# Attention scores in a two-layer encoder kernel: 64-row products become 128-row products

## The chip, the cores and the metric

The kernel runs on one core of one Trainium2 chip. The metric is the device time of one execution in microseconds; lower is better. Before the change three runs gave 1617.46 us in the median (1617.28 to 1620.55).

## What is computed

Two consecutive layers of an encoder over 512 tokens of width 1024. Each layer mixes tokens in three branches, A (neighbourhood attention on an 8 x 64 grid, 6 heads), B (dilated attention, 3 groups of 2 heads) and M (attention into 256 memory tokens, 4 heads), gates and merges them, and then runs a gated MLP with a short convolution. The heads have 64 features. Cut to what matters:

```python
proj = h @ w_in[l]
q_a, k_a, v_a, q_b, k_b, v_b, q_m, gate_pre = jnp.split(proj, splits, axis=-1)
s = jnp.einsum('bhqd,bhrqcd->bhqrc', q_row, k_win) * scale      # A: 8 x 16 neighbours, plus bias
s = jnp.einsum('bhqd,bhqkd->bhqk', qq, kk) * scale + alibi       # B: one group of heads
s = jnp.einsum('bshd,bmhd->bhsm', qh, km) * (HEAD_DIM ** -0.5)   # M
merged = gates[..., 0, :] * (o_a @ w_br_a[l]) + gates[..., 1, :] * (o_b @ w_br_b[l]) + gates[..., 2, :] * (o_m @ w_br_m[l])
x = x + rms_norm(merged @ w_out[l], g_post_mix[l])
u = depthwise_conv_centred(rms_norm(x, g_pre_ffn[l]) @ w_up[l], conv_w[l], conv_b[l])
a, b = jnp.split(u, 2, axis=-1)
x = x + rms_norm((jax.nn.gelu(a) * b) @ w_down[l], g_post_ffn[l])
```

## The kernel before

Activations lie with features on partitions and the 512 tokens along the free axis, in tiles of 128x512. Nearly every product is made in float32 accuracy from operands in two parts, a high part (float32r) and a low part (the rest): high by high, high by low, low by high. So a linear layer over 1024 features is 24 matmuls for each 128 outputs (`linear`, `mm3`). Each weight tile is loaded by SP, its high part is cast by ScalarE (ACT) and its low part is subtracted by VectorE (DVE) or GpSimd (POOL).

Two heads of 64 features share a tile of 128 partitions, rows 0 to 63 and 64 to 127. For the scores, `stack_split` keeps for each head one query tile whose high part lies on the head's own 64 partitions and whose low part lies on the other 64. `twice_split` keeps for each head one key tile with the high part on both halves (the second half is copied by POOL), and one tile for both heads with the low parts, each on its own half. `mm_stacked` (line 265) then makes a score in two matmuls into the same PSUM bank:

```python
mm(ps, q, k, True, False, cost)     # 128 rows: (high q, low q) by (high k, high k)
mm(ps, qh, kl, False, True, cost)   # 64 rows: high q by low k
```

It is called in `a_head_job` (line 529; two blocks of two pairs for each head, 256 keys each), in `m_head_job` (two blocks of two pairs for each head, 256 keys) and in `b_job` (four blocks for each head, one pair over 512 keys). In `b_job` two more score products in plain float32 stand behind the pair, one for each strided group, over 64 rows and 128 keys (`mm1`); their queries are one tile for both heads, made in `b_q` (line 576).

The order of PE is one stream. `Woven` holds a main stream (the linear layers, one K tile at a time) and jobs beside it (heads, transposes, norms); a job's next part is issued into the main stream as soon as a rough count of the time so far says that its operands should be ready. The order is fixed when the program is built: `Woven.pe` makes every matmul depend on the one before. The counts take a matmul's columns, not its rows, so a switch between shapes has no place in them.

Buffers: `mp` has 35 tiles of 128x512 (tag m), for merged branches, attention operands, the first w_up weights and the MLP's activations; tag `ka` has 9 tiles, for branch A's keys, branch M's queries, the first w_out weights and the MLP's last activations. A new tile waits until the last reader of the buffer's former tile is done. PSUM has eight banks: three for the linear layers (mm), two for scores (s), two for transposes (pt), one for outputs (o). At the end of a sub-layer (`sublayer_end`) the last products are made half by half of the tokens, and the norm of the first half runs beside the products of the second; meanwhile the first six weights of w_up are loaded and split into tiles of `mp` (`group_weights`, low parts on POOL).

Of the kernel before, what the change touches and what calls it, by code (L numbers as in the profile page):

```python
# [16 lines left out]
N_MEM = 256  # L17
# [13 lines left out]
# columns of the per-feature vectors  # L31
# [14 lines left out]
class Woven:  # L46
    """Issue order of the tensor engine: one main stream, and beside it jobs whose parts come as soon
    as the other engines should have their operands ready (by a rough count of the time so far)."""
# [50 lines left out]
class Counted:  # L99
    """An engine, with a rough count of when it is done with what it was given so far."""  # L100
# [19 lines left out]
def tile_hybrid_encoder(ctx, tc, xT, memT, memg, vecs, rpb, w_in, w_kv, w_bra, w_brb, w_brm,  # L120
# [6 lines left out]
    mp = ctx.enter_context(tc.tile_pool(name="mp", bufs=35))  # L127
# [22 lines left out]
    def ktile(dt=F32R, shape=(128, 512)):  # L150
        return tp.tile(list(shape), dt, tag="ka", name=nm("ka"), bufs=9)
# [63 lines left out]
    def behind(ins, other):  # L215
        """Issue ins behind other, of the same engine."""
        if other is not None and ins is not other:
            tc.add_manual_dep(ins, other.name, ORDER, reason="issue order")
# [5 lines left out]
    def weights(src, K, C, slot=None, eng=None, after=None):  # L224
        """An operand of weights in two parts: a list over its K tiles."""
        raw = wp.tile([128, K, C], F32, tag="wraw", name=nm("wraw"))
        nc.sync.dma_start(out=raw, in_=src)
        if slot is None:
            hi = wp.tile([128, K, C], F32R, tag="whi", name=nm("whi"), bufs=2)
            lo = wp.tile([128, K, C], F32R, tag="wlo", name=nm("wlo"), bufs=2)  # L230
            split(raw, hi, lo, eng)
            behind(last_copy[0], after)
            return [(hi[:, k, :], lo[:, k, :]) for k in range(K)]
        n = 512 // C
        w = []
        for k in range(0, K, n):
            c = min(n, K - k)
            hi, lo = slot(F32R, (128, c, C)), slot(F32R, (128, c, C))
            split(raw[:, k:k + c, :], hi, lo, eng)
            w += [(hi[:, i, :], lo[:, i, :]) for i in range(c)]  # L240
        return w
# [23 lines left out]
    def mm_stacked(ps, q, k, qh, kl, n):  # L265
        """q k in float32's accuracy: high and low part of q on top of each other, against the high part of k
        twice, and the high part of q against the low part of k."""
        cost = n / 2400.0
        mm(ps, q, k, True, False, cost)
        mm(ps, qh, kl, False, True, cost)  # L270
# [8 lines left out]
    def stack_split(ps, tiles, scale=None, pv=lambda t: t, tv=lambda t: t):  # L279
        """One tile for each of the two heads in ps: high part on the head's partitions, low part on the others."""  # L280
        for t, row in zip(tiles, (0, 64)):
            part(tv(t[row:row + 64]), tv(t[64 - row:128 - row]), pv(ps[row:row + 64]), scale)

    def twice_split(ps, tiles, lo, scale=None, eng=None):
        """The high part of each of the two heads in ps on both halves of its tile, and the low parts in lo."""
        for t, row in zip(tiles, (0, 64)):
            a = t[row:row + 64]
            part(a, lo[row:row + 64], ps[row:row + 64], scale)
            if eng is None:
                ACT.activation(t[64 - row:128 - row], ps[row:row + 64], AF.Copy, scale=scale or 1.0)  # L290
            else:
                eng.tensor_copy(t[64 - row:128 - row], a)
# [31 lines left out]
    def rstd_job(accs, n, box):  # L324
        """1 / sqrt(mean of squares + eps) of each token, on all partitions (in PSUM)."""
        nb = n // 128
        bank = tbank((128, n + nb))
        pr, pt = bank[:, 0:n], bank[:, n:n + nb]
        for i, a in enumerate(accs):
            for b in range(nb):  # L330
                mm(pt[:, b:b + 1], a[:, 128 * b:128 * b + 128], mean, i == 0 and b == 0,
                   i == len(accs) - 1 and b == nb - 1, 0.11)
        rs = smalls(nb)
        crit[0] = ACT.activation(rs, pt, AF.Sqrt, bias=eps, scale=1.0).ins
        V.reciprocal(rs, rs)
        diag = small("h32", 4, (128, n))
        for b in range(nb):
            V.tensor_scalar_mul(diag[:, 128 * b:128 * b + 128], ident, rs[:, b:b + 1])
        yield 1.2
        mm(pr, ones, diag, True, True, n * 4 / 2400.0)  # L340
        box.append(pr)
# [67 lines left out]
    def mem_kv(l, hm, km, vm, pre=()):  # L409
        wv.need(f"mem{l}")  # L410
        kl = big(F32R, (128, 2, N_MEM))
        for m in range(4):
            w = pre[m] if pre else weights(w_kv[l, m], KD, 128)
            ps = mmbank((128, N_MEM))
            linear(ps, w, hm, slice(0, N_MEM))
            if m < 2:
                t = big(F32R, (128, 2, N_MEM))
                twice_split(ps, (t[:, 0, :], t[:, 1, :]), kl[:, m, :], None, MDUP)
                km.append((t, kl[:, m, :]))
            else:  # L420
                vT = big(F32, (128, 256))
                ACT.copy(vT, ps)
                wv.spawn(mem_v_job(l, vT, vm))

# [26 lines left out]
    def v_split(srcs):  # L451
        """Values of four tiles of keys: for each tile and head the high part beside the low part."""
        ps = tbank((128, 2, 2, 2, 64))
        transposes(ps.rearrange("p a b c d -> p (a b c d)"), srcs)
        out = []
        for a in range(2):
            t = big(F32R, (128, 2, 2, 2, 64))
            split(ps[:, a], t[:, :, :, 0, :], t[:, :, :, 1, :])
            out += [[t[:, b, c] for c in range(2)] for b in range(2)]
        return out  # L460

    def mm_values(po, v, p, cols, first, last, n, view=lambda t: t):
        """Adds v p to the columns of po: high and low part of v against the high part of p (in two halves of
        partitions), and the high part of v against the low part of p."""
# [32 lines left out]
    def a_k(ps, qkv):  # L497
        kk = [ktile(F32R, (128, 528)) for _ in range(3)]
        for t in kk:
            nc.gpsimd.tensor_copy(t[:, 0:8], zero)  # L500
            nc.gpsimd.tensor_copy(t[:, 520:528], zero)
        twice_split(ps, [t[:, 8:520] for t in kk[:2]], kk[2][:, 8:520], -0.125, DUP)
        qkv[1].append(kk)

    def a_v(ps, qkv, flag):
        # columns rolled by 8, then cut in tiles of 16 columns
# [8 lines left out]
    def kwin(t, b):  # L515
        # columns 16 b - 8 to 16 b + 23 of each row, in the order (tile, row, column)
# [12 lines left out]
    def a_head_job(l, h, qkv, neg, oa):  # L529
        qs, ks, vs = qkv  # L530
        pr, row = h // 2, 64 * (h % 2)
        q, k, kl = qs[pr][h % 2], ks[pr][h % 2], ks[pr][2][row:row + 64, :]
        P = []
        for bp in range(2):
            s = sbank((128, 2, 256))
            for b2 in range(2):
                b = 2 * bp + b2
                qsl = slice(128 * b, 128 * b + 128)
                mm_stacked(s[:, b2, :], q[:, qsl], kwin(k, b), q[row:row + 64, qsl], kwin(kl, b), 256)
# [36 lines left out]
    def b_q(g, ps, qkv):  # L576
        if g > 0:
            t = big(F32)
            ACT.activation(r3(t), b_cls(ps), AF.Copy, scale=-0.125)
            qkv[0].append(t)  # L580
            return
# [4 lines left out]
    def b_k(g, ps, qkv):  # L586
# [5 lines left out]
        kk = [big() for _ in range(3)]  # L592
        twice_split(ps, kk[:2], kk[2], None, DUP)
# [10 lines left out]
    def b_job(l, sl, cp, qkv, po, ob):  # L604
# [3 lines left out]
        for c2 in range(2):  # L608
# [4 lines left out]
            mm_stacked(s0, qs[0][sl][:, rsl], ks[0][sl], qs[0][sl][row:row + 64, rsl], ks[0][2][row:row + 64, :], 512)  # L613
# [4 lines left out]
            for g in (1, 2):  # L618
                mm1(s1[:, g - 1, :], qs[g][row:row + 64, rsl], ks[g][row:row + 64, rsl], True, True, 128)
# [42 lines left out]
    def m_head_job(l, h, qm, km, vm, om):  # L662
        pr, row = h // 2, 64 * (h % 2)
        q, (kt2, kl) = qm[pr][h % 2], km[pr]
        P = []
        for qp in range(2):
            s = sbank((128, 2, 256))
            for q2 in range(2):
                qsl = slice(128 * (2 * qp + q2), 128 * (2 * qp + q2) + 128)
                mm_stacked(s[:, q2, :], q[:, qsl], kt2[:, h % 2, :], q[row:row + 64, qsl], kl[row:row + 64, :], 256)  # L670
# [69 lines left out]
    def sublayer_end(l, goff, w_of, rhs, n_half, then, lat=(1.4, 1.8), mid=None):  # L740
        """A sub-layer's last linear layer and its norm. The last n_half output tiles are made half by
        half: the norms of the first half run beside the products of the second."""
# [63 lines left out]
    for l in range(depth):  # L806
# [52 lines left out]
        for j in range(NFF):  # L859
# [13 lines left out]
            hi, lo = (big if j < 18 else ktile)(), (big if j < 17 else ktile)()  # L873
# [45 lines left out]
def _consts():  # L919
# [4 lines left out]
    # query (i, cc) of column block b; key (t, r, c): column 16 (b + t) - 8 + c  # L924
# [24 lines left out]
def _layout(inputs):  # L949
# [19 lines left out]
    # relative position bias by query (i, cc) and key (t, r, c); columns out of the table padded  # L969
# [40 lines left out]
```

## Time and profile before

| | |
|---|---|
| runs, median (lowest to highest) | 1617.46 us (1617.28 to 1620.55) |
| span of the profiled execution | 1616.8 us |
| layer 0: attention, branches A, B, M | 82 to 270 us |
| layer 0: gates and branch projections | 270 to 392 us |
| layer 0: w_out, norm, first w_up tiles | 392 to 462 us |
| layer 1: attention | 880 to 1068 us |
| mean granted TensorE clock | 0.990 |

The span goes from the first to the last instruction of the one profiled execution; the runs' times hold some 0.7 us around it. A row of instructions by form gives line, engine, operation, tile written and tiles read, rows*columns of the weight, shape of the moving operand, count, then busy time in us and mean duration in ns of one. Matmuls overlap, so the mean duration of one is longer than the distance from one start to the next. All matmuls have line 244, as one helper records them; their tiles tell them apart: s are scores, pt transposes, o outputs of attention, mm linear layers. A row in order of time gives start, duration, engine, line, operation, tiles and count.

### The profile page before, as it was taken

The page shows a single profiled execution, that of the slowest core. Times are in us where ns is not written, and L with a number is a line of the kernel's source. Part 1 is how long each engine was busy: PE and PEld are TensorE (multiplying, and loading weights), DVE is VectorE, ACT ScalarE, POOL GpSimd, SP SyncE. Part 2 cuts the span into 40 slices and gives each one's busy share as a digit, 9 for nine tenths or more (in the row PEclk, how much of TensorE's full clock was granted, in tenths as well). Part 3 has the DMA queues.
Part 4 walks back from the last instruction along what each step waited for, and adds up shares of the span by engine and source line. Part 5 has one row for each costly group of instructions (what it writes and reads, how often), then busy time and mean ns, then how long its engine had stood idle before and what let it go on. Part 6 is the DMA issues. An engine that isn't in the chain of part 4 may idle for free.

```text
span 1616.8 us, 21319 instructions
## 1 busy us (share of the span) xinstructions
PE 1571.7 (97%) x8246; PEld 1331.6 (82%) x8246; DVE 916.9 (57%) x1654; ACT 726.2 (45%) x1285; POOL 165.9 (10%) x200
## 2 busy tenths in 40 slices
PE   6999999999999999999989999999999999999997
PEld 5977877889898888878888787778898888888887
DVE  6676566335676565542386746653448665655233
ACT  5455566235444444432344545652354544444231
POOL 4230000110300000010151300001112000000000
PEclk9999999999999999999999999999999999999998
DMA  7221212324202223333331211132331123232331
GB/s 236 85 76 58 67 55 64 111 78 157 79 27 95 100 92 104 112 92 97 121 103 46 76 62 63 48 103 79 104 131 66 53 93 104 91 105 85 98 107 63
DMA packets 46614, 144.95 MB, mean 90 GB/s; under 512 B 5233, under 2 KB 11377, under 8 KB 46513
## 3 DMA queue, kind: packets, MB, share of 16 engines
q1 hardware_dynamic: 44656, 139.61, 26.3%
q10 hardware_dynamic: 1152, 2.10, 0.5%
q0 software_dynamic: 704, 1.88, 0.4%
q8 instruction: 65, 1.06, 0.3%
q14 instruction: 37, 0.30, 0.1%
HBM read 141.47 MB, written 2.10 MB: 89 GB/s over the span
## 4 chain that ended last, share of the span: by engine, by line
PE 92%; DVE 5%; ACT 1%; issue 1%; DMA 0%; SPq 0%; ACTq 0%
PE mm L244 75%; PE s L244 9%; PE o L244 4%; PE pt L244 3%; PE pt L255 2%; DVE h L114 1%; DVE y L114 1%; DVE x L114 1%; DVE acc L114 1%; DMA x<-in_xT_dram 0%; DVE wlo L114 0%; ACT whi L114 0%; ACT sq L114 0%; DVE m L114 0%; ACT y L114 0%
## 5 line engine op out<-in xcount | busy, mean ns | idle before, releaser
L244 PE MATMUL mm<-h,whi 128*128 128x512 f32 x2432 | 758.5, 393 | 0.0
L244 PEld LDWEIGHTS mm<-h,whi 128*128 128x128 f32 x2432 | 449.2, 188 | 93.5
L114 DVE TENSOR_TENSOR wlo<-wraw,whi 128x1024 fp32r<-128x1024 f32 (+1 forms) x203 | 247.4, 1220 | 401.9 <-ACT whi L114 398.2
L244 PE MATMUL mm<-h,wlo 128*128 128x512 f32 x1216 | 473.8, 390 | 0.0
L114 ACT CAST whi<-wraw 128x1024 fp32r<-128x1024 f32 (+1 forms) x203 | 210.4, 1039 | 306.1 <-PE mm L244 301.7
L244 PEld LDWEIGHTS mm<-h,wlo 128*128 128x128 f32 x1216 | 228.3, 188 | 48.8
L244 PE MATMUL mm<-m,whi 128*128 128x512 f32 (+1 forms) x711 | 192.8, 358 | 1.6 <-DVE m L114 0.8
L244 PEld LDWEIGHTS mm<-m,whi 128*128 128x128 f32 x711 | 128.4, 194 | 20.7 <-PE mm L244 1.3
L244 PE MATMUL mm<-m,wlo 128*128 128x512 f32 (+1 forms) x362 | 128.9, 356 | 0.7 <-DVE wlo L114 0.7
L114 DVE SCALAR_TENSOR_TENSOR y<-mm,vec,y 128x511 f32<-128x511 f32 x160 | 118.9, 747 | 8.5 <-ACT y L114 5.9
L114 ACT ACTIVATE y<-mm,vec 128x512 f32<-128x512 f32 (+1 forms) x163 | 113.6, 698 | 0.1
L244 PE MATMUL mm<-m,m 128*128 128x512 f32 (+1 forms) x432 | 89.2, 347 | 0.0
L727 POOL TENSOR_TENSOR m<-m,y 128x512 f32<-128x512 f32 x28 | 36.1, 1288 | 466.1 <-DVE y L114 466.1
L222 POOL TENSOR_TENSOR m<-wraw,m 128x512 fp32r<-128x512 f32 x42 | 57.1, 1374 | 242.4 <-ACT m L114 182.7
L244 PEld LDWEIGHTS mm<-m,wlo 128*128 128x128 f32 x362 | 70.1, 194 | 10.4 <-DVE wlo L114 1.1
L244 PEld LDWEIGHTS mm<-m,m 128*128 128x128 f32 x432 | 67.6, 189 | 9.1
L244 PE MATMUL mm<-h,m 128*128 128x256 f32 x456 | 66.0, 303 | 5.5 <-ACT y L114 2.3
L114 DVE TENSOR_TENSOR acc<-acc,sq 128x256 f32<-128x256 f32 (+1 forms) x86 | 47.2, 551 | 36.9 <-ACT sq L114 36.2
L244 PEld LDWEIGHTS mm<-h,m 128*128 128x128 f32 x456 | 61.4, 206 | 8.1 <-ACT h L114 2.7
L114 ACT ACTIVATE y<-y 128x512 f32<-128x512 f32 x44 | 27.9, 633 | 87.3 <-DVE y L114 87.3
L114 ACT CAST m<-wraw 128x512 fp32r<-128x512 f32 (+1 forms) x98 | 56.1, 602 | 22.0 <-DMA wraw<-in_w_brb_dram 9.7
L114 ACT CAST m<-y 128x512 fp32r<-128x512 f32 x36 | 22.4, 621 | 87.7 <-DVE y L114 87.7
(148 smaller groups left out, 1835.9 us busy)
## 6 DMA issues: line engine op xcount, KB each, us to landing
wraw<-in_w_in_dram SPq DMA_DIRECT2D x88, 512.0 KB, 3.2
wraw<-in_w_up_dram SPq DMA_DIRECT2D x88, 512.0 KB, 3.2
wraw<-in_w_down_dram SPq DMA_DIRECT2D x32, 512.0 KB, 3.5
wraw<-in_w_out_dram SPq DMA_DIRECT2D x16, 512.0 KB, 3.3
wraw<-in_w_down_dram SPq DMA_DIRECT2D x16, 384.0 KB, 3.1
wraw<-in_w_kv_dram SPq DMA_DIRECT2D x8, 512.0 KB, 3.5
wraw<-in_w_bra_dram SPq DMA_DIRECT2D x16, 192.0 KB, 2.3
x<-in_xT_dram SPq DMA_DIRECT2D x8, 256.0 KB, 7.0
```

Of the source, the lines that this page charges most:

```text
L114: return op(*args, **kw)
L222: last_lo[eng or V] = (eng or V).tensor_sub(lo, src, f32(hi)).ins
L244: wv.pe(nc.tensor.matmul(ps, a, b, start=first, stop=last), cost)
L255: wv.pe(nc.tensor.transpose(ps[:, 128 * i:128 * i + 128], s, ident), 0.11)
L727: (V if br == 2 and m >= 6 else G).tensor_add(acc[m], acc[m], gs)
```

## The change

The low part of the keys gets a tile of its own for each head, with the same values on both partition halves, as the high part has it. The second matmul of `mm_stacked` then takes the whole query tile (high and low part) instead of its 64 high rows: 128 rows by 128 rows. It adds low q by low k, which was left out before. For the strided groups of branch B each head gets a query tile of its own whose other 64 rows are zero, so that these products too run over 128 rows; the keys stay one tile for both heads. The buffers are shared out anew: 32 tiles in `mp`, 12 under `ka`, and the MLP's activations from tile 16 on lie under `ka`. Comments are dropped too.

```diff
-    mp = ctx.enter_context(tc.tile_pool(name="mp", bufs=35))
+    mp = ctx.enter_context(tc.tile_pool(name="mp", bufs=32))
...
-        return tp.tile(list(shape), dt, tag="ka", name=nm("ka"), bufs=9)
+        return tp.tile(list(shape), dt, tag="ka", name=nm("ka"), bufs=12)
...
-    def mm_stacked(ps, q, k, qh, kl, n):
+    def mm_stacked(ps, q, kh, kl, n):
         cost = n / 2400.0
-        mm(ps, q, k, True, False, cost)
-        mm(ps, qh, kl, False, True, cost)
+        mm(ps, q, kh, True, False, cost)
+        mm(ps, q, kl, False, True, cost)
...
-    def twice_split(ps, tiles, lo, scale=None, eng=None):
-        for t, row in zip(tiles, (0, 64)):
-            a = t[row:row + 64]
-            part(a, lo[row:row + 64], ps[row:row + 64], scale)
-            if eng is None:
-                ACT.activation(t[64 - row:128 - row], ps[row:row + 64], AF.Copy, scale=scale or 1.0)
-            else:
-                eng.tensor_copy(t[64 - row:128 - row], a)
+    def twice_split(ps, his, los, scale=None, eng=None):
+        for hi, lo, row in zip(his, los, (0, 64)):
+            own, other = slice(row, row + 64), slice(64 - row, 128 - row)
+            part(hi[own], lo[own], ps[own], scale)
+            eng.tensor_copy(hi[other], hi[own])
+            eng.tensor_copy(lo[other], lo[own])
...
     def a_k(ps, qkv):
-        kk = [ktile(F32R, (128, 528)) for _ in range(3)]
+        kk = [ktile(F32R, (128, 528)) for _ in range(4)]
...
     def b_q(g, ps, qkv):
         if g > 0:
-            t = big(F32)
-            ACT.activation(r3(t), b_cls(ps), AF.Copy, scale=-0.125)
-            qkv[0].append(t)
+            tiles = (big(F32), big(F32))
+            for t, row in zip(tiles, (0, 64)):
+                G.memset(t[64 - row:128 - row, :], 0.0)
+                ACT.activation(r3(t[row:row + 64]), b_cls(ps[row:row + 64]), AF.Copy, scale=-0.125)
+            qkv[0].append(tiles)
...
-                mm1(s1[:, g - 1, :], qs[g][row:row + 64, rsl], ks[g][row:row + 64, rsl], True, True, 128)
+                mm1(s1[:, g - 1, :], qs[g][sl][:, rsl], ks[g][:, rsl], True, True, 128)
...
-            hi, lo = (big if j < 18 else ktile)(), (big if j < 17 else ktile)()
+            hi, lo = (big if j < 16 else ktile)(), (big if j < 16 else ktile)()
```

On PE nothing changes its place. These are the rows of the first score block of branch B in layer 0 (s is the score bank, the first m behind the arrow the keys, the second the queries), before:

```order
L244 MATMUL s_1863<-m_1318,m_1209 128x512
L244 MATMUL s_1863<-m_1320,m_1209 128x512
L244 MATMUL s_1869<-m_1590,m_1518 128x128
L244 MATMUL s_1869<-m_1785,m_1752 128x128
L244 MATMUL mm_1894<-h_110,whi_1890 128x512
```

and with the change:

```order
L244 MATMUL s_1894<-m_1338,m_1229 128x512
L244 MATMUL s_1894<-m_1340,m_1229 128x512
L244 MATMUL s_1900<-m_1617,m_1541 128x128
L244 MATMUL s_1900<-m_1816,m_1779 128x128
L244 MATMUL mm_1925<-h_110,whi_1921 128x512
```

The sizes are those of what is written, so the rows read the same; the second, third and fourth product now take 128 rows in place of 64.

On POOL, around the last biases of branch A's heads in layer 0 (rpb are the bias tables, L526 makes a head's bias, L292 copies the keys of branch B), before:

```order
L292 COPY m_1318<-m_1318 64x512
L526 TENSOR_TENSOR y_1371<-mask,y_1371 128x256
L292 COPY m_1319<-m_1319 64x512
L523 DMA y_1495<-in_rpb_dram 128x256
L526 TENSOR_TENSOR y_1494<-mask,y_1495 128x256 x2
```

and with the change (L290 copies the high part, L291 the low part, L579 fills with zeros):

```order
L290 COPY m_1338<-m_1338 64x512
L525 TENSOR_TENSOR y_1394<-mask,y_1394 128x256
L291 COPY m_1340<-m_1340 64x512
L290 COPY m_1339<-m_1339 64x512
L291 COPY m_1341<-m_1341 64x512
L522 DMA y_1518<-in_rpb_dram 128x256
L525 TENSOR_TENSOR y_1517<-mask,y_1518 128x256 x2
L525 TENSOR_TENSOR y_1518<-mask,y_1518 128x256
L579 MEMSET m_1541 64x512
L579 MEMSET m_1542 64x512
```

Behind each copy of a high part now stands one of a low part, and the fills for branch B's queries come behind the last bias.

On ACT, in the second half of w_out of layer 0 (sq and y belong to the norm that follows w_out, m<-wraw are casts of weights), before:

```order
L114 ACTIVATE sq_831_3764<-mm_3739 128x256
L114 ACTIVATE y_3603<-mm_3739,vec 128x256
L114 CAST m_4235<-wraw_4233 128x512
L114 CAST m_4239<-wraw_4233 128x512
L114 ACTIVATE sq_833_3793<-s_3768 128x256
```

and with the change:

```order
L114 ACTIVATE sq_846_3911<-mm_3886 128x256
L114 ACTIVATE y_3638<-mm_3886,vec 128x256
L114 ACTIVATE sq_848_3940<-s_3915 128x256
L114 ACTIVATE y_3639<-s_3915,vec 128x256
L114 CAST m_4266<-wraw_4264 128x512
L114 ACTIVATE st_3966<-pt_3963,eps 128x2
L114 CAST m_4270<-wraw_4264 128x512
```

The casts of the first w_up weight moved behind the sums of squares of w_out's tiles, to the first norm's square root, and the other w_up weights move back by as much.

More of the change, by code (lines that the diff above doesn't have):

```diff
@@ L410, in mem_kv @@
         wv.need(f"mem{l}")
-        kl = big(F32R, (128, 2, N_MEM))
         for m in range(4):
@@ L416, in mem_kv @@
             if m < 2:
-                t = big(F32R, (128, 2, N_MEM))
-                twice_split(ps, (t[:, 0, :], t[:, 1, :]), kl[:, m, :], None, MDUP)
-                km.append((t, kl[:, m, :]))
+                t, u = big(F32R, (128, 2, N_MEM)), big(F32R, (128, 2, N_MEM))
+                twice_split(ps, (t[:, 0, :], t[:, 1, :]), (u[:, 0, :], u[:, 1, :]), None, MDUP)
+                km.append((t, u))
             else:
@@ L501, in a_k @@
             nc.gpsimd.tensor_copy(t[:, 520:528], zero)
-        twice_split(ps, [t[:, 8:520] for t in kk[:2]], kk[2][:, 8:520], -0.125, DUP)
+        inner = [t[:, 8:520] for t in kk]
+        twice_split(ps, inner[:2], inner[2:], -0.125, DUP)
         qkv[1].append(kk)
@@ L531, in a_head_job @@
         pr, row = h // 2, 64 * (h % 2)
-        q, k, kl = qs[pr][h % 2], ks[pr][h % 2], ks[pr][2][row:row + 64, :]
+        q, k, kl = qs[pr][h % 2], ks[pr][h % 2], ks[pr][2 + h % 2]
         P = []
@@ L538, in a_head_job @@
                 qsl = slice(128 * b, 128 * b + 128)
-                mm_stacked(s[:, b2, :], q[:, qsl], kwin(k, b), q[row:row + 64, qsl], kwin(kl, b), 256)
+                mm_stacked(s[:, b2, :], q[:, qsl], kwin(k, b), kwin(kl, b), 256)
             S = ytile((128, 2, 256))
@@ L591, in b_k @@
             return
-        kk = [big() for _ in range(3)]
-        twice_split(ps, kk[:2], kk[2], None, DUP)
+        kk = [big() for _ in range(4)]
+        twice_split(ps, kk[:2], kk[2:], None, DUP)
         qkv[1].append(kk)
@@ L612, in b_job @@
             s0 = sbank()
-            mm_stacked(s0, qs[0][sl][:, rsl], ks[0][sl], qs[0][sl][row:row + 64, rsl], ks[0][2][row:row + 64, :], 512)
+            mm_stacked(s0, qs[0][sl][:, rsl], ks[0][sl], ks[0][2 + sl], 512)
             m0, m1 = smalls(1), smalls(1)
@@ L663, in m_head_job @@
         pr, row = h // 2, 64 * (h % 2)
-        q, (kt2, kl) = qm[pr][h % 2], km[pr]
+        q, (kh, kl) = qm[pr][h % 2], km[pr]
         P = []
@@ L669, in m_head_job @@
                 qsl = slice(128 * (2 * qp + q2), 128 * (2 * qp + q2) + 128)
-                mm_stacked(s[:, q2, :], q[:, qsl], kt2[:, h % 2, :], q[row:row + 64, qsl], kl[row:row + 64, :], 256)
+                mm_stacked(s[:, q2, :], q[:, qsl], kh[:, h % 2, :], kl[:, h % 2, :], 256)
             m = smalls(2)
```

## The prediction

> **What bounds the kernel now.** I read the page first (busy time, chain), then the windows of the attention stages, then PE's products by form, then the order of time around single score blocks.
>
> ```profile
> span 1616.8 us, 21319 instructions
> PE 1571.7 (97%) x8246; PEld 1331.6 (82%) x8246; DVE 916.9 (57%) x1654; ACT 726.2 (45%) x1285; POOL 165.9 (10%) x200
> PE 92%; DVE 5%; ACT 1%; issue 1%; DMA 0%; SPq 0%; ACTq 0%
> 82.00:160.00 78.00, 77.91 (x378) 61.04 (x379) 54.26 (x146) 43.06 (x98) 15.67 (x19) 1.00 0.19 66
> 160.00:235.00 75.00, 75.00 (x384) 59.84 (x383) 42.08 (x104) 41.31 (x75) 0.00 (x0) 1.00 0.19 62
> 235.00:270.00 35.00, 35.00 (x156) 25.62 (x155) 24.63 (x59) 24.25 (x53) 0.00 (x0) 1.00 0.17 52
> ```
>
> The reader is to see that PE (TensorE) is the bound: 97% busy, 92% of the chain that ended last. The three windows (columns: length, then busy time of PE, PEld, DVE, ACT, POOL, then granted clock and DMA) are branches A, B and M of layer 0's attention; layer 1 repeats them. PE has no gap there, the clock is 1.00, and VectorE (DVE) is at 70%, 56% and 70%. So time taken off PE in these stages comes off the span, until a wait takes its place.
>
> But a busy PE need not be PE at its rate. By form, over the whole program:
>
> ```profile
> L244 PE MATMUL s<-h,m 128*128 128x256 f32 x384 | 49.0, 287 | 0.0
> L244 PE MATMUL s<-ka,m 128*128 128x256 f32 x48 | 16.5, 344 | 0.0
> L244 PE MATMUL s<-ka,m 64*128 64x256 f32 x48 | 18.3, 382 | 0.0
> L244 PE MATMUL s<-m,ka 64*128 64x256 f32 x32 | 12.2, 381 | 0.0
> L244 PE MATMUL s<-m,m 64*128 64x512 f32 x16 | 7.9, 495 | 0.0
> L244 PE MATMUL s<-m,m 64*128 64x128 f32 x64 | 9.9, 274 | 0.0
> ```
>
> A product of 256 columns takes 287 ns where all have 128 rows (first row); the score products of 64 rows take 381 and 382, and in branch A their 128-row partners 344. Fewer rows cost more, and the neighbour pays too. That is the sign of a switch between 64-row and 128-row products, not of an operand.
>
> **What a switch costs.** Three blocks of scores in the order of time (start, duration), one for each branch, with the products of the main stream behind them; under them two rows that give the undisturbed rates.
>
> ```profile
> 83.79 1.23 PE L244 MATMUL s<-ka,m 128*128 128x256 f32 x4
> 84.94 0.73 PE L244 MATMUL mm<-h,whi 128*128 128x512 f32 x2
> 85.52 0.40 PE L244 MATMUL mm<-h,wlo 128*128 128x512 f32 x1
> ...
> 174.34 1.27 PE L244 MATMUL s<-m,m 128*128 128x512 f32 x6
> 175.53 0.73 PE L244 MATMUL mm<-h,whi 128*128 128x512 f32 x2
> 176.11 0.39 PE L244 MATMUL mm<-h,wlo 128*128 128x512 f32 x1
> ...
> 235.36 1.21 PE L244 MATMUL s<-m,ka 128*128 128x256 f32 x4
> 236.50 0.72 PE L244 MATMUL mm<-h,whi 128*128 128x512 f32 x2
> 237.07 0.40 PE L244 MATMUL mm<-h,wlo 128*128 128x512 f32 x1
> ```
> ```profile
> 157.68 14.29 PE mm L244 x63
> 447.27 5.76 PE s L244 x48
> ```
>
> Undisturbed, a product of 512 columns starts each 14.29/63 = 0.227 us, and one of 256 each 5.76/48 = 0.120. For 128 columns: the 64 records above stand in 16 runs of four, so (9.9 - 16 x 0.274)/48 = 0.115 from one to the next.
>
> - Branch A: four score products and the two behind them take 85.52 - 83.79 = 1.73; undisturbed 4 x 0.120 + 2 x 0.227 = 0.93. Excess 0.80, four switches, 0.20 each.
> - Branch M: 237.07 - 235.36 = 1.71 against 0.93. Excess 0.78.
> - Branch B, whose 64-row products stand together: 176.11 - 174.34 = 1.77 against 2 x 0.227 + 4 x 0.115 + 2 x 0.227 = 1.37. Excess 0.40, two switches.
>
> **The change, part by part.** All score products get 128 rows, in the same order on PE. The 48, 32 and 16 products of the rows above are 24 blocks of A and 16 of M (two such products each) and 16 of B (one). Taken off PE: 24 x 0.80 + 16 x 0.78 + 16 x 0.40 = 19.2 + 12.5 + 6.4 = **38.1 us**. That a 128-row product with as many columns costs no more follows from the first row against those of 64 rows; I take the difference as nothing, and what is left of an operand's own cost is inside the spread of 0.02 between A and M.
>
> The measured 0.20 us has a rule beside it. The Trainium skill, TensorEngine Tiling (Array Packing), Key Properties, says that a change of tiling mode drains the TensorE, and the Trainium skill, TensorE: Matmul & The Clock Gate, Single matmul latency, gives a constant of 166 ns at full clock that a stream of matmuls hides. An estimate by that figure of the Trainium skill: 24 x 4 + 16 x 4 + 16 x 2 = 192 switches x 0.166 = 31.9 us and a time of 1589; by the rows above it is 38.1, and these decide.
>
> A rule also speaks against the change. The Trainium skill, TensorEngine Tiling (Array Packing), When to Use Tiling, would split a contraction of up to 64 into row tiles that run together; an estimate by it: the 80 products of 256 columns could at best halve, 80 x 0.120 / 2 = 4.8 us, and padding gives this up. The trace shows no two of them side by side, so nothing is lost here.
>
> *Copies and zeros on POOL.* Per layer 8 copies of 64x512, 4 of 64x256, 4 fills of 64x512 and 6 small casts come in.
>
> ```profile
> L292 POOL CAST ka<-ka 64x512 fp32r<-64x512 f32 x12 | 7.6, 632 | 65.5 <-ACT ka L114 65.4
> L292 POOL CAST m<-m 64x512 fp32r<-64x512 f32 x4 | 4.2, 1053 | 3.7 <-ACT m L114 3.5
> 49.40 0.61 POOL L292 CAST ka<-ka 64x512 fp32r<-64x512 f32 x1 [0.67 <-ACT ka L114]
> ```
>
> Copies cost 0.63 to 1.05 us each; a fill has no row of its size, so from nothing to 1.05. Together at most 22 x 1.05 = 23 us a layer on an engine with 15.7 us of work in the first 78 us and none in the next 110. A pair's copies come long before their use (49.40 against the first score at 83.79), so I cost them at nothing. Without that cover, one copy late is about 1 us of PE. The two extra ACT instructions a layer for the queries (about 1 us each at most, by the 64x512 rows above) lie in a stage with ACT at 55%.
>
> *Three buffers fewer in the pool of 128x512 tiles.* With 35, one w_up weight was split while w_out still ran; with 32 (16 merged tiles and 16 of w_out fill the pool) POOL's first subtractions must wait.
>
> ```profile
> 397.60 1.30 POOL L222 TENSOR_TENSOR m<-wraw,m 128x512 fp32r<-128x512 f32 x1 [22.10 <-ACT m L114]
> 410.77 1.28 POOL L222 TENSOR_TENSOR m<-wraw,m 128x512 fp32r<-128x512 f32 x1 [11.88 <-DVE acc L114]
> 437.69 4.17 POOL L222 TENSOR_TENSOR m<-wraw,m 128x512 fp32r<-128x512 f32 x3 [11.48 <-PE mm L244]
> 452.87 0.52 PE L244 MATMUL o<-h,m 128*128 128x256 f32 x3
> ```
>
> The one of 397.60 moves behind 410.77, and one more joins the three at 437.69: done by 437.7 + 4 x 1.39 = 443.3. Queued behind are only the other w_up subtractions, whose last pair is read from 452.87 on: 9 us of cover, so nothing; uncovered it would cost at most the slip, 13 us a layer. Of ACT's casts that move with them, two land next to the norm that follows w_out: between nothing and, by POOL's row, 1.3 us each; I take nothing, as ACT is at 45% overall.
>
> **What is late next.** The scores have two PSUM banks, which VectorE empties. In branch B it is already late:
>
> ```profile
> 184.97 1.27 PE L244 MATMUL s<-m,m 128*128 128x512 f32 x6
> 187.31 1.48 PE L244 MATMUL s<-m,m 128*128 128x512 f32 x6
> 210.06 1.37 PE L244 MATMUL s<-m,m 128*128 128x512 f32 x6
> 185.54 0.69 DVE L114 TENSOR_TENSOR m<-pt,m 128x512 fp32r<-128x512 f32 x1
> 186.15 0.68 DVE L114 CUSTOM_DVE_ANT_0 y<-s,tab 128x512 f32<-128x512 f32 x1
> 186.87 0.69 DVE L114 SCALAR_TENSOR_TENSOR ka<-mm,ka 64x512 fp32r<-64x512 f32 x1
> 187.59 0.42 DVE L114 CUSTOM_DVE_ANT_0 y<-s,tab 128x256 f32<-128x256 f32 x1
> ```
>
> The same six products take 1.27, then 1.48 and 1.37 us, since they wait for the second reading of a bank (187.59), with VectorE busy without a break before it. Between those two blocks the saving (0.40, and half of the next block's, 0.2) turns into a wait at 187.31, and half as much at 210.06: 0.9 us a layer. In branch M VectorE's 24.63 us will stand in 35 - 8 x 0.78 = 28.8 (86%), ScalarE's 24.25 too (84%); I put 0.9 us a layer there, an estimate between nothing and the whole 6.2. Given back in all: 2 x 1.8 = **3.6 us**.
>
> **Sum.** 38.1 - 3.6 = 34.5 us. Span 1616.8 becomes 1582.3; the runs' median, 1617.46, lies 0.7 above the span, so 1583.0.
>
> **Rivals.**
> 1. *VectorE and ScalarE take PE's place in A and M.* For: 86% and 84% dense in M, and the softmax of one head must end before its transposes. Against: no wait there now, and both have over 4 us idle left in M. If half the saving of A and M turned into waits: (19.2 + 12.5)/2 + 1.8 = 17.7 given back, 1597 us.
> 2. *The change doesn't do what it says*: the excess belongs to the second product of an accumulation, not to its rows. Then nothing is gained: 1617 to 1618. Against: the 128-row product behind a block pays as well, and B's row of 64-row products runs at 0.115 inside.
> 3. *Slower: the granted clock falls* as PE loses its pauses in the attention stages, 2 x 187 - 38 = 336 us of PE. It decides from a clock of 336/(336 + 34.5) = 0.91 on; at 0.85 it costs 59 us, 1642 us. Against: the clock is 1.00 where PE is full, and lower where it has gaps:
>
> ```profile
> 427.00:462.00 35.00, 33.53 (x249) 32.70 (x250) 25.09 (x65) 14.43 (x41) 4.10 (x3) 0.91 0.09 31
> ```
>
> **Chances.** Forecast (given back 0 to 8 us, 1579 to 1587) 0.81; rival 1 (1588 to 1606) 0.13; rival 2 0.03; rival 3 0.03. Faster by over 0.2%, which is about what can be told from no change: 0.94; within it 0.03; slower 0.03. The range goes from 1577 (nothing given back, 1579.4, less 2 us for the 0.02 to 0.04 by which 56 blocks may differ) to 1596, which takes in most of rival 1.
>
> **What would show it.** No form with 64 rows among the scores; 256-column scores at 0.28 to 0.29 us as in the first row; a block in A or M of 0.93 us up to the third product behind it. Layer 0's attention 17 to 19 us shorter. The waits that come in stand ahead of the scores in B, released by VectorE. POOL's w_up subtractions start near 411, with the first w_up products not later than before against the norm. Wrong would be: scores of 128 rows that still take over 0.34 us; a clock under 1.00 in attention; gaps of PE in A or M that sum to over 8 us.

## The result, and the profile after

The changed kernel took 1578.80 us in the median (1578.59 to 1579.04), the kernel before, on the same chip, 1617.37: a ratio of 0.9757 with a 95% interval from 0.9738 to 0.9775. The predicted 1583.0 us lay 4.2 us above. The profiled execution took 1579.04 us, with a span of 1577.3.

The page of the profile after: the span, the busy times, and the shares of the chain that ended last.

```profile
span 1577.3 us, 21375 instructions
PE 1529.7 (97%) x8246; PEld 1316.4 (83%) x8246; DVE 911.2 (58%) x1654; ACT 727.4 (46%) x1289; POOL 186.4 (12%) x244
PE 88%; DVE 8%; ACT 2%; issue 1%; DMA 1%; SPq 0%; ACTq 0%
```

The span fell by 39.5 us and PE's busy time by 42.0, with as many matmuls. PE still bounds the kernel, but its share of the chain went from 92% to 88%, and DVE's from 5% to 8%: some of what PE gave up is now waiting.

The windows of branches A, B and M of layer 0 after the change. They are cut where the same matmuls start as at 82, 160, 235 and 270 us before, so the length (second column) compares with 78, 75 and 35.

```profile
81.27:150.20 68.93, 68.83 (x378) 58.67 (x379) 54.48 (x146) 43.86 (x100) 20.64 (x27) 1.00 0.23 74
150.20:222.93 72.73, 71.92 (x384) 59.57 (x383) 41.85 (x104) 41.32 (x75) 0.00 (x0) 1.00 0.21 63
222.93:253.27 30.34, 29.27 (x156) 24.00 (x155) 24.35 (x59) 24.44 (x53) 0.00 (x0) 1.00 0.21 61
```

A is 9.07 us shorter, B 2.27, M 4.66: 16.0 us in layer 0. Layer 1, cut in the same way, is 15.9 us shorter. PE's busy time fell by 9.08, 3.08 and 5.73; where a length fell by less than that, PE now waits, 0.81 us in B and 1.07 us in M.

The scores by form, over the whole program (column in the middle: busy us, mean ns).

```profile
L244 PE MATMUL s<-ka,m 128*128 128x256 f32 x96 | 15.9, 288 | 0.0
L244 PE MATMUL s<-m,ka 128*128 128x256 f32 x160 | 24.8, 284 | 0.0
L244 PE MATMUL s<-m,m 128*128 128x512 f32 x32 | 10.3, 404 | 0.7 <-DVE st L114 0.7
L244 PE MATMUL s<-m,m 128*128 128x128 f32 x64 | 9.9, 277 | 0.9 <-DVE st L114 0.9
```

No score has 64 rows any more. Of branch A's keys (ka) the second products took 382 ns and the first 344; now all 96 take 288. The 64-row products of 512 columns took 495; now all 32 of that size take 404.

The same three blocks in the order of time, after the change, each with the third product behind it.

```profile
83.05 0.64 PE L244 MATMUL s<-ka,m 128*128 128x256 f32 x4
...
83.99 0.39 PE L244 MATMUL mm<-h,wlo 128*128 128x512 f32 x1
...
164.51 1.06 PE L244 MATMUL s<-m,m 128*128 128x512 f32 x6
...
165.87 0.39 PE L244 MATMUL mm<-h,wlo 128*128 128x512 f32 x1
...
223.38 0.63 PE L244 MATMUL s<-m,ka 128*128 128x256 f32 x4
...
224.31 0.39 PE L244 MATMUL mm<-h,wlo 128*128 128x512 f32 x1
```

From the block's start to the third product behind it A takes 0.94 us, B 1.36 and M 0.93. The prediction had reckoned 0.93, 1.37 and 0.93 for blocks without a switch.

Outside the attention stages the span fell by another 39.5 - 31.9 = 7.6 us, for which the prediction had nothing. (In a second pair of profiles, at the end of the next section, this is 4.9.) The next section takes both parts apart.

### The profile page after: what moved, and what is told of

The parts are those of the page before. It is cut to its first block, busy times and chain, and to the rows that moved or that the text cites. A ratio compares the mean times of both kernels' runs of the same rounds, so it can differ in the third digit from the quotient of the medians.

```text
span 1577.3 us, 21375 instructions
## 1 busy us (share of the span) xinstructions
PE 1529.7 (97%) x8246; PEld 1316.4 (83%) x8246; DVE 911.2 (58%) x1654; ACT 727.4 (46%) x1289; POOL 186.4 (12%) x244
## 4 chain that ended last, share of the span: by engine, by line
PE 88%; DVE 8%; ACT 2%; issue 1%; DMA 1%; SPq 0%; ACTq 0%
PE mm L244 73%; PE s L244 6%; PE o L244 3%; PE pt L244 2%; DVE h L114 2%; PE pt L255 2%; DVE y L114 2%; DVE x L114 1%; DVE m L114 1%; DVE wlo L114 1%; ACT whi L114 1%; DVE acc L114 1%; DVE ka L114 0%; ACT y L114 0%; DMA m<-in_memT_dram 0%
## 5 line engine op out<-in xcount | busy, mean ns | idle before, releaser
L244 PE MATMUL mm<-m,whi 128*128 128x512 f32 (+1 forms) x672 | 178.2, 354 | 1.6 <-DVE m L114 0.8
L244 PEld LDWEIGHTS mm<-m,whi 128*128 128x128 f32 x672 | 119.6, 192 | 19.0 <-PE mm L244 1.3
L244 PE MATMUL mm<-m,wlo 128*128 128x512 f32 (+1 forms) x336 | 118.3, 352 | 0.7 <-DVE wlo L114 0.7
L244 PEld LDWEIGHTS mm<-m,wlo 128*128 128x128 f32 x336 | 64.4, 192 | 9.4 <-DVE wlo L114 1.1
L114 ACT CAST m<-pt 128x512 fp32r<-128x512 f32 (+1 forms) x72 | 38.2, 539 | 40.4 <-PE pt L255 32.0
```

What stands on the lines that cost most here:

```text
L114: return op(*args, **kw)
L244: wv.pe(nc.tensor.matmul(ps, a, b, start=first, stop=last), cost)
```

## The experiments

"Gain" is counted against the kernel before, 1617 to 1619 us in each set of runs. Stage lengths are measured between the starts of the same matmuls in two traces.

**The second product on 64 rows again.** The changed kernel, but the low part of the keys is multiplied with the high part of the queries alone (qr, 64 rows), as before; low q by low k is left out. Buffers, copies and padded queries of the strided groups stay.

```diff
-        mm(ps, q, kl, False, True, cost)
+        mm(ps, qr, kl, False, True, cost)
```

> This kernel is the changed one with its copies, zeros and buffers, but the second product of every score pair takes 64 rows again (low query by low key is left out, as before). Theory 1, each switch between 64-row and 128-row products costs 0.20 us of TensorE: A and M have four switches a block again and B two, so attention is as long as before, 16 us more in each layer, and the time is 1611 us (1608 to 1614), since what the change gained outside attention stays. Rival, the gain comes from the new buffers or from where the copies stand: 1579 to 1583 us.

Measured: 1611.38 us, ratio 0.9956 (0.9940 to 0.9971). Each branch of both layers is within 0.2 us of its length before, and the old duration is back:

```profile
L244 PE MATMUL s<-ka,m 64*128 64x256 f32 x48 | 18.4, 383 | 0.0
```

So the whole gain inside attention needs the second product on 128 rows; what is left, 5.8 us, lies outside attention.

**The buffers alone.** The kernel before with the new sizes of the pools and nothing else.

```diff
-    mp ... bufs=35
+    mp ... bufs=32
...
-        ... tag="ka", ... bufs=9)
+        ... tag="ka", ... bufs=12)
...
-            hi, lo = (big if j < 18 else ktile)(), (big if j < 17 else ktile)()
+            hi, lo = (big if j < 16 else ktile)(), (big if j < 16 else ktile)()
```

> The kernel before with the buffers of the changed one (32 tiles in mp, 12 under ka, the MLP's last activations under ka) and nothing else. Theory 1: attention keeps its length (branches A, B and M 188 us in each layer); only the norm behind w_out moves, as GpSimd's subtractions start later: its wait at 427.6 falls from 3.4 to about 2.3 us, time 1612 to 1617 us. Rival, the buffers carry the gain: 1579 to 1590 us.

Measured: 1613.78 us, ratio 0.9972 (0.9958 to 0.9986). Attention keeps its length; most of what moved lies in the w_out stages and at the layer boundary. The profiled execution was the fastest of the ten (1610.05 us), with a mean granted clock of 0.996 against 0.990 in the profile before, so part of its gain is clock. At one mean clock, 0.994, two of these runs have spans of 1610.3 and 1610.4 us and two of the kernel before 1612.5 and 1613.3: some 2.5 us that the clock does not explain. So the new buffer sizes alone made the kernel a little faster. The run changes both pools; which of the two matters is not shown.

**Half as many switches.** The kernel before with its 64-row products kept, but in A and M a block's two 128-row products stand together and then its two 64-row ones: two switches a block where there were four. The cut shows A; M is changed in the same way.

```diff
             for b2 in range(2):
                 b = 2 * bp + b2
-                qsl = slice(128 * b, 128 * b + 128)
-                mm_stacked(s[:, b2, :], q[:, qsl], kwin(k, b), q[row:row + 64, qsl], kwin(kl, b), 256)
+                mm(s[:, b2, :], q[:, 128 * b:128 * b + 128], kwin(k, b), b2 == 0, False, 256 / 2400.0)
+            for b2 in range(2):
+                b = 2 * bp + b2
+                mm(s[:, b2, :], q[row:row + 64, 128 * b:128 * b + 128], kwin(kl, b), False, b2 == 1, 256 / 2400.0)
...
```

> The kernel before, but in each block of branches A and M the two 128-row products come first and then the two 64-row ones: as many 64-row products, two switches in place of four. Theory 1: 40 blocks x 2 x 0.20 = 16 us less, with 2 to 4 us given back to VectorE: 1604 us (1600 to 1607). Rival, a 64-row product is slow by itself or the second product of a pair pays: no gain, 1615 to 1619 us.

Measured: 1601.36 us, ratio 0.9890 (0.9870 to 0.9911). Branch A's first block, and the windows of A, B and M of layer 0, in this kernel:

```profile
83.97 0.83 PE L244 MATMUL s<-ka,m 128*128 128x256 f32 x4
...
85.29 0.40 PE L244 MATMUL mm<-h,wlo 128*128 128x512 f32 x1
```
```profile
82.18:155.65 73.47, 73.38 (x378) 59.92 (x379) 54.23 (x146) 43.00 (x98) 15.69 (x19) 1.00 0.20 70
155.65:230.59 74.94, 74.94 (x384) 59.73 (x383) 42.08 (x104) 41.20 (x75) 0.00 (x0) 1.00 0.18 61
230.59:262.65 32.06, 32.06 (x156) 24.93 (x155) 24.46 (x59) 24.22 (x53) 0.00 (x0) 1.00 0.19 62
```

The block's excess is 85.29 - 83.97 - 0.93 = 0.39 us in place of 0.80. A is 4.53 us shorter and M 2.94, half of the PE time that the change takes off there (9.08 and 5.73), and B, which was not touched, keeps its length. The same products with half the switches cost half the excess: it belongs to the switch, neither to the 64 rows as such nor to the second product of an accumulation. Per switch taken away that is 4.53/24 = 0.19 us in A and 2.94/16 = 0.18 in M.

**The strided groups on 64 rows again.** The changed kernel without the padded queries of branch B.

```diff
-                mm1(s1[:, g - 1, :], qs[g][sl][:, rsl], ks[g][:, rsl], True, True, 128)
+                mm1(s1[:, g - 1, :], qs[g][row:row + 64, rsl], ks[g][row:row + 64, rsl], True, True, 128)
```

> The changed kernel, but the strided groups of branch B keep one query tile and 64 rows, as before. Theory 1: a block of B has its two switches again, so branch B is as long as before, 2.3 to 2.6 us more in each layer: 1583.6 us (1582.5 to 1585). Rival, the rows count and not the switches: the 64-row products of 512 columns are gone all the same, so a third to half of B's gain stays, 1581 to 1582 us.

Measured: 1584.06 us, ratio 0.9786 (0.9759 to 0.9813). Branch B of layer 0 in this kernel:

```profile
151.91:226.82 74.91, 74.87 (x384) 59.62 (x383) 42.02 (x104) 41.21 (x75) 0.00 (x0) 1.00 0.18 61
```

A and M keep their whole gain (9.07 and 4.65 us in layer 0) and B's is gone (75.00 to 74.91): the switch had only moved, from in front of the second product to behind it. So each branch's gain is its own, and B needs all its scores on 128 rows to get anything.

**Later issue in B and in M.** What PE waits for after the change, in layer 0 (releasers: st is written where VectorE reads the score bank, y and m are the softmax and its split; the row of 235.12 shows the two products just before a wait).

```profile
177.39 0.71 PE L244 MATMUL s<-m,m 128*128 128x128 f32 x4 [0.45 <-DVE st L114]
...
235.12 0.63 PE L244 MATMUL o<-m,m 128*128 128x512 f32 x2
236.31 0.68 PE L244 MATMUL o<-m,m 128*64 128x512 f32 x2 [0.57 <-DVE m L114]
...
251.94 0.59 PE L255 MATMUL pt<-ident,y 128*128 128x128 f32 x2 [0.50 <-DVE y L114]
```

With one more wait of 0.36 us in B these are the whole 1.9 us. Two kernels put the waiting steps 0.6 us (B) and 0.7 us (M) later in the planner's count, and a third does both.

```diff
-            yield LAT_QK if c2 == 0 else ready(LAT_SM)     # B
+            yield 1.6 if c2 == 0 else ready(LAT_SM)
...
-            yield LAT_QK if qp == 0 else ready(LAT_SM)     # M
+            yield LAT_QK if qp == 0 else ready(5.2)
-            yield ready(LAT_T2) if kt == 0 else ready(LAT_T)
+            yield ready(LAT_T2) if kt == 0 else ready(2.2)
```

> The kernel after the change, with the second score block of a B part issued 0.6 us later in the planner's count (1.6 for 1.0), all else as after. Theory 1 (what B gives back is TensorE's wait for VectorE ahead of the second block, 0.45 and 0.36 us in each layer at 177.39 and 199.19 of the profile after, and other work can be put there): these two waits go in both layers, B is 0.6 to 0.8 us shorter in each, 1577.2 to 1577.6 us. Rival (the engines behind B set its pace, a later issue only moves the wait): the waits come up at a later step of the same part, 1578.5 to 1579.3 us.

> The kernel after the change, with M's transposes and value products issued 0.7 us later in the planner's count (5.2 for 4.5 and 2.2 for 1.5), all else as after. Theory 1 (M gives back what TensorE waits at 236.31 and 251.94 in the profile after, 0.57 and 0.50 us, in each layer): both waits go, M is about 1.0 us shorter in each layer, 1576.7 to 1577.2 us. Rival (VectorE and ScalarE set M's pace): they come back at later heads of M, 1578.5 to 1580 us.

> The kernel after the change with both of these later issues. If both are waits that other work can fill: 1575.2 to 1576.5 us, under every other kernel here. If either is only moved: 1577 to 1580 us.

Measured: 1579.91 us (ratio 0.9764, 0.9749 to 0.9780), 1580.45 (0.9771, 0.9757 to 0.9784) and 1582.18 (0.9778, 0.9765 to 0.9791); none is faster than the changed kernel. All three lie above what theory 1 asked for, the first two by some 0.5 us above the rival's ranges as well, and the third above both of its ranges. The waits in the first two:

```profile
216.15 0.55 PE L255 MATMUL pt<-ident,y 128*128 128x128 f32 x3 [0.60 <-DVE y L114]
```
```profile
240.05 0.68 PE L244 MATMUL o<-m,m 128*64 128x512 f32 x2 [0.65 <-DVE m L114]
...
259.76 0.93 PE L244 MATMUL o<-m,m 128*128 128x512 f32 x3 [1.40 <-DVE m L114]
```

In B the waits of 0.45 and 0.36 us went and one of 0.60 came up in front of later transposes, which leaves 0.2 us; up to the end of attention each layer is 0.4 us shorter, where theory 1 had asked for 0.6 to 0.8, and the time does not show it. For M's heads the waits grew from 1.07 to 2.05 us a layer. The rival holds in M and mostly in B: a later issue moves these waits. That 24.35 us of VectorE and 24.44 of ScalarE stand in 30.34 us of M fits that, but which of the two sets the pace wasn't tried.

**GpSimd beside the norm.** The gain outside attention starts at the norm behind w_out. There, VectorE adds to the residual (x), and PE waits for the sum of the squares. First VectorE's rows of before, and what POOL does then:

```profile
414.48 1.85 DVE L114 TENSOR_TENSOR x<-x,y 128x256 f32<-128x256 f32 x2
416.26 0.74 DVE L114 TENSOR_TENSOR y<-y,pt 128x256 f32<-128x256 f32 x2
```
```profile
414.51 4.41 POOL L222 TENSOR_TENSOR m<-wraw,m 128x512 fp32r<-128x512 f32 x3 [0.54 <-PE mm L244]
```

Then the same additions of after, and POOL's rows there:

```profile
397.25 0.75 DVE L114 TENSOR_TENSOR x<-x,y 128x256 f32<-128x256 f32 x2
```
```profile
394.13 1.28 POOL L222 TENSOR_TENSOR m<-wraw,m 128x512 fp32r<-128x512 f32 x1 [35.62 <-ACT m L114]
396.01 1.29 POOL L222 TENSOR_TENSOR m<-wraw,m 128x512 fp32r<-128x512 f32 x1 [0.60 <-ACT m L114]
397.87 2.74 POOL L222 TENSOR_TENSOR m<-wraw,m 128x512 fp32r<-128x512 f32 x2 [0.57 <-ACT m L114]
```

After the change POOL is idle from 397.30 to 397.87, and the two additions fall mostly into that. Beside POOL they took 1.10 us more. PE's wait for the sum, in before, after, and the kernel with the buffers alone:

```profile
427.61 0.98 PE L244 MATMUL pt<-mean,acc 128*128 128x1 f32 x4 [3.41 <-DVE acc L114]
```
```profile
409.29 0.58 PE L244 MATMUL pt<-mean,acc 128*128 128x1 f32 x4 [2.32 <-DVE acc L114]
```
```profile
424.59 0.58 PE L244 MATMUL pt<-mean,acc 128*128 128x1 f32 x4 [2.32 <-DVE acc L114]
```

It fell by 1.09 us, and by as much with the buffers alone. To test the reading from both sides, one kernel puts more POOL work beside this norm (t are 512 columns of a table, multiplied by ones), and one takes all of it away:

```diff
+                at = G.tensor_sub(idle, acc[:, half][:, 0:64], mask[:, 0, 0:64]).ins
+                for _ in range(4):
+                    behind(G.tensor_tensor(out=t, in0=t, in1=<ones>, op=ALU.mult).ins, at)
```
```diff
-        gw = group_weights([w_up[l, m] for m in up], (G,) * 6)
+        gw = group_weights([w_up[l, m] for m in up], (V,) * 6)
```

> The kernel after the change, with five more GpSimd operations in each layer (one of 64 columns and four of 512) put beside the first norm after w_out, on data that nothing needs changed; their results are what was there already. Theory 1 (VectorE's additions take 1.5 us in place of 0.41 where GpSimd works beside them, so what GpSimd does beside this norm costs TensorE's wait): GpSimd is busy some 5 us more beside the norm, VectorE's chain to the sum of squares is 2 to 4 us longer in each layer, TensorE's wait for it goes from 2.32 to 4 to 6 us, 1582.5 to 1587 us. Rival (the shorter wait after the change has another cause): the wait stays at 2.3 us, 1578 to 1580 us.

> The kernel after the change, with the twelve subtractions for the first six w_up weights of each layer on VectorE in place of GpSimd, all else as after; GpSimd is idle beside the norm after w_out. Theory 1 (GpSimd's work beside it slows VectorE): VectorE's additions take 0.41 us each there, the chain from the first product with the norm's factor to the sum of squares, 13.7 us after the change, loses five slow additions of 1.1 us and gets some three subtractions of about 0.6 us, so it is some 3.5 us shorter though VectorE does more; TensorE's wait of 2.32 us for that sum goes to below 0.5 us in each layer; later subtractions give up to 1.5 us back at the next wait: 1574 to 1579 us. Rival (no slowing, VectorE has only more to do): that wait grows to about 4.3 us, 1582 to 1586 us.

Measured with more POOL work: 1586.34 us, ratio 0.9798 (0.9785 to 0.9811). The same two pairs of additions and PE's wait:

```profile
398.23 2.59 DVE L114 TENSOR_TENSOR x<-x,y 128x256 f32<-128x256 f32 x2
...
402.18 2.95 DVE L114 TENSOR_TENSOR x<-x,y 128x256 f32<-128x256 f32 x2
```
```profile
413.17 0.99 PE L245 MATMUL pt<-mean,acc 128*128 128x1 f32 x4 [5.22 <-DVE acc L114]
```

The wait grew by 2.9 us in each layer. In layer 0 the clock fell as well (0.91 from 404 to 442 us, 1.00 in the changed kernel), so not all of the longer time is the slowed VectorE. Measured without POOL work: **1569.51 us**, ratio 0.9706 (0.9692 to 0.9719). The same rows, and the window from 404 to 442 us:

```profile
397.09 0.75 DVE L114 TENSOR_TENSOR x<-x,y 128x256 f32<-128x256 f32 x2
...
398.76 0.75 DVE L114 TENSOR_TENSOR x<-x,y 128x256 f32<-128x256 f32 x2
...
406.65 0.50 PE L244 MATMUL pt<-mean,acc 128*128 128x1 f32 x4
```
```profile
404.00:442.00 38.00, 37.06 (x303) 36.33 (x302) 30.77 (x83) 20.10 (x53) 0.00 (x0) 1.00 0.20 70
```

Every addition is at its short duration, the sum is there when PE comes (no wait in the row), and PE is busy for 37.06 of 38 us, though VectorE does more. The forecast of 1574 to 1579 was too careful: I had put up to 1.5 us back at the next wait, and that wait shrank as well, from 1.47 to 0.34 us at the product with the norm's factors (pt<-h,ones). Against the changed kernel run beside it (below, 0.9766) this is 9.5 us, and it beats both kernels. Of it 4.1 us lie in layer 0's w_out stage, measured between the starts of the same matmuls, with the clock at 1.00 in both; how much of the rest is clock was not separated.

**Both of the better edits.**

> Both the subtractions on VectorE and the second score block of B 0.6 us later, all else as after. By theory 1 of each: some 1 us under the run before it by the lengths of the stages, 1573 to 1578 us; the granted clock's halves after waits can hide as much. By the rivals: 1582 us or more.

Measured: 1569.84 us, ratio 0.9707 (0.9694 to 0.9721). The later issue in B adds nothing that can be told.

**Both kernels once more.**

> The kernel after the change once more, unchanged. Theory 1 (where the clock falls to half for 3.4 or 6.8 us is set by how a fixed grid of 3.4 us lies to the run, and differs between runs of one kernel): stretches at half clock at other places or in another number than in the first profile, where one lies at 1186, and its TensorE waits the same to 0.1 us; 1577 to 1584 us. Rival (the change itself took the half clock away): the profile shows the same single stretch, 1578.6 to 1579.1 us.

> The kernel before the change once more, unchanged. Theory 1 as for the run before it: other stretches at half clock than the five of the first profile (27, 426, 822, 836 and 1225 us); 1613 to 1623 us with the same TensorE waits. Rival: the same five places.

Measured: after 1579.06 us (1578.48 to 1579.89), ratio 0.9766 (0.9753 to 0.9779); before 1616.32 us, one run. PE's waits repeat to 0.1 us at the norm (2.33 and 3.40). The granted clock (third column from the right) in windows of 16 to 32 and 404 to 442 us: first before and before again, then after and after again.

```profile
16.00:32.00 16.00, 13.20 (x78) 12.74 (x79) 12.85 (x28) 9.04 (x24) 5.85 (x5) 0.89 0.67 220
404.00:442.00 38.00, 34.59 (x266) 34.19 (x265) 26.60 (x52) 19.03 (x49) 15.31 (x11) 0.91 0.21 70
```
```profile
16.00:32.00 16.00, 13.98 (x85) 13.52 (x84) 12.50 (x28) 9.64 (x26) 5.84 (x5) 0.89 0.71 240
404.00:442.00 38.00, 34.60 (x262) 34.19 (x262) 26.48 (x52) 18.67 (x48) 15.31 (x11) 0.91 0.20 70
```
```profile
16.00:32.00 16.00, 13.66 (x89) 13.33 (x89) 13.10 (x28) 8.70 (x22) 5.86 (x6) 1.00 0.69 228
404.00:442.00 38.00, 33.47 (x269) 32.39 (x269) 29.19 (x71) 16.77 (x45) 9.30 (x7) 1.00 0.17 56
```
```profile
16.00:32.00 16.00, 13.42 (x82) 13.00 (x83) 12.38 (x27) 9.41 (x25) 5.85 (x5) 0.89 0.69 230
404.00:442.00 38.00, 33.46 (x269) 32.39 (x268) 29.18 (x70) 16.77 (x45) 9.54 (x7) 1.00 0.16 56
```

At the start the clock differs between two executions of one kernel (1.00 and 0.89), as theory 1 has it. At the norm it doesn't: half-clock time of 0.09 x 38 / 0.5 = 6.8 us in both of before, none in both of after. Neither theory holds alone. The other stretches lie near their old places, with other lengths in the kernel before: from 1180 to 1236 us the clock is 0.94 and 0.97 in the two profiles of before, 0.94 in both of after. The clock lost at the start does not show in the span: it is 1577.3 us in both profiles of after.

## Why the prediction came out as it did

The time was inside the range and 4.2 us faster than forecast. By the spans, 1582.3 was forecast and 1577.3 came: 2.6 us less gained inside attention, 7.6 us more outside.

1. *PE is the bound and a switch costs its time.* Right, and shown: with the switches put back the gain in attention goes, with half of them away half of the gain in A and M comes.
2. *The gross saving of 38.1 us.* The mechanism was right and the size about 1 us too large. Matched block by block, from a block's start to the second product behind it, A's 24 blocks save 18.5 us (0.77 each, 0.80 forecast), M's 16 save 12.3 (0.77, 0.78 forecast), and B's save 0.39 each where no wait falls into them (0.40 forecast), which makes 6.2: 37.0 in all. A block with transposes behind it saves only 0.72 to 0.74. The Trainium skill's 166 ns (TensorE: Matmul & The Clock Gate, Single matmul latency) would have made 31.9. 37.0/192 gives 0.193 us a switch, nearer to the rows than to that figure.
3. *Given back: 3.6 us.* It was 37.0 - 31.9 = 5.1, so this term was 1.5 us too small: together with the 1 us above, the 2.6 that were missing in attention. PE's idle time in the windows, 1.9 us in each layer (B 0.81, M 1.07; 0.9 stood for each), shows less than a wait costs, because a product counts as busy for some 0.39 us where the next could start after 0.227. Around the wait at 236.31 the row shows 0.57 us idle; but four such products took 0.92 us from their start to the next scores before the change (250.21 to 251.13) and take 1.71 there (235.12 to 236.83), 0.79 more. For the same reason PE's busy time in the six windows fell by only 17.9 + 17.8 = 35.7. In B the waits stand where the prediction put them, at the two blocks that were late before (187.31 and 210.06, now 177.39 and 199.19), released by VectorE. M's place was only estimated, and its transposes and outputs wait, not its scores.
4. *POOL's copies and fills cost nothing.* Right: POOL's busy time rose from 165.9 to 186.4 us, and in branch A, where it works beside attention, PE has no new wait (68.83 busy of 68.93, 77.91 of 78.00 before).
5. *Three buffers fewer cost nothing.* **This is the step that failed**, in sign. The timing was right: POOL's first subtraction moved behind the first norm's start (394.13, where 397.60 would have been some 380 on the new clock), and PE did not wait for it. But I asked only who waits for POOL, not whom POOL slows. With the subtractions moved, one fewer falls on VectorE's chain of additions, and PE's wait falls by 1.1 us in each layer. At the layer boundary the same happens, with the order of POOL's subtractions and small casts changed. VectorE, then PE, first before, then after:

```profile
817.19 1.48 DVE L114 TENSOR_TENSOR x<-x,y 128x256 f32<-128x256 f32 x1
...
819.87 0.62 PE L244 MATMUL mm<-h,m 128*128 128x256 f32 x3 [2.31 <-ACT y L114]
```
```profile
797.37 0.41 DVE L114 TENSOR_TENSOR x<-x,y 128x256 f32<-128x256 f32 x1
...
798.98 0.38 PE L244 MATMUL mm<-h,m 128*128 128x256 f32 x1 [0.65 <-ACT y L114]
```

   ACT's square waits for that addition, PE's bank for ACT: 1.66 us. With the buffers alone PE's wait there is 0.66 us too. These three waits make 1.09 + 1.10 + 1.66 = 3.85 of the 7.6 us. Against them stand new waits of 1.47 and 0.89 us right behind the norms.

   The rest, 7.6 - 3.85 + 2.36 = 6.1 us, I put down to the granted clock, for which the prediction had no term outside attention. PE's busy time outside attention fell by 42.0 - 35.7 = 6.3 us with as many matmuls, and the clock lost up to 8.5 us less after the change: (1 - granted clock) times length, summed over four windows at the start, the two norms and the boundary, is 11.8 us before and 3.4 after (1.8 of the difference lie at the start, where two profiles of after differ by as much and have one span). That is a sum that fits, not an experiment.

   The runs at one mean clock give a second view: at 0.994 the two spans of before are 1612.5 and 1613.3 us and the five of after 1576.8 to 1578.0, on the mean 35.6 apart. Without attention's 31.9 that leaves 3.7 us, about half of the 7.6, that is not clock, as much as the three waits make. The new waits would then belong to the clock's part, as what PE loses by reaching the norm's factors sooner; that is not shown.
6. *The rivals.* VectorE and ScalarE did not take PE's place: PE is busy for 29.27 of 30.34 us in M. The change does what it says. The clock stayed at 1.00 in all six attention windows.

So 1583.0 was near partly by luck: the gain in attention was 2.6 us too large, a gain of 7.6 us was not seen at all, and the two misses have opposite signs. What stays open is what decides whether the clock falls at a given wait, and so how much of the clock's part belongs to the change.

## What to carry to other kernels

Rows that differ in duration without differing in work point to what stands between them: compare the distance from a block's start to the products behind it with the undisturbed rate. Price a wait in the same way, from start to start: the idle time in a profile row can be less. If products of 64 and 128 rows alternate, padding to 128 (or, without any new data, grouping those of one height) can cost less than the switches. When an edit moves work on GpSimd, look for two-input VectorE work beside its new and its old place, even where nothing waits for GpSimd; here moving twelve subtractions a layer to the busier engine was worth 9.5 us. And compare kernels at the same granted clock before giving a small difference to an edit.

## What the hardware showed unexpectedly

- **VectorE beside GpSimd.** An addition of two 128x256 fp32 tiles in SBUF takes 0.41 us with POOL idle and 1.48 us beside a POOL subtraction, and a pair takes 0.75 us, 1.85 where one of the two is held up, or 2.59 to 2.95 where both are. Multiplications of the same size with one input in PSUM (y<-y,pt) took 0.74 us a pair in the same stretch. The Trainium skill, SBUF — State Buffer, SBUF: two separate sides, has a rule for this: the two engines share one pair of ports, and a VectorE instruction with two SBUF inputs and a GpSimd one that reads SBUF lock each other out for a whole instruction. The traces agree, down to the PSUM input being left alone.
- **The clock after waits.** Behind waits PE's clock fell to half. A window inside such a stretch of the kernel before (clock third from the right):

```profile
427.00:433.00 6.00, 5.39 (x23) 5.25 (x24) 3.34 (x10) 3.46 (x12) 0.00 (x0) 0.50 0.00 0
```

  The time at half clock is a multiple of one length: (1 - 0.89) x 16 / 0.5 = 3.5 us in the window at the start, 6.8 us at the norm. The Trainium skill, TensorE: Matmul & The Clock Gate, What's actually happening, gives a free-running window of 3413 ns for it; the lengths agree, and so does the start of one kernel being at 1.00 once and at 0.89 once. That layer 0's norm of before lost it in both profiles and that of after in neither is not explained by it alone, and the length of the wait seems to have a say. The two norms behind w_out in all fourteen profiles make 28 cases: with a wait of 3.4 or 5.2 us (eight) the clock fell every time, with 2.3 us (sixteen) in ten, without a wait (four) never. So a wait of 2.3 us may or may not cost it: with the strided groups on 64 rows again, and with the later issue in B, layer 0's norm has after's wait of 2.32 us and a clock of 0.91 from 404 to 442 us.
- **A switch between 64 and 128 rows** costs TensorE 0.18 to 0.20 us on the mean of a branch, also within one accumulation and with the same query columns, and the product behind pays as well as the switched one.
